# Column sums on the vector engines for two modulation banks, rows spread by DMA, C blocks without context

## The chip, the core and the metric

The kernel runs on one core of a Trainium2 chip. The core has five engines with a queue each: TensorE (PE in the profile, with its weight loads as PEld), VectorE (DVE), ScalarE (ACT), GpSimd (POOL) and SyncE (SP), which here only issues DMAs. ACT and POOL issue some DMAs too. Each engine works through its queue in order and waits at semaphores for the others. The metric is the device time of one execution in microseconds. Before the change the median of three runs is 1828.47 us (1827.12 to 1831.48).

## The reference

One layer of a hybrid diffusion backbone in float32, with 512 latent tokens `x`, 256 context tokens `ctx` and model width 1024. What matters here is the modulation, the projection and the convolution:

```python
mod = jax.nn.silu(c) @ ada_w[i] + ada_b[i]
sh1, sc1, g1, sh2, sc2, g2 = jnp.split(mod[:, None, :], 6, axis=-1)
mod_c = jax.nn.silu(c_ctx) @ ada_w[i] + ada_b[i]
csh1, csc1, cg1, csh2, csc2, cg2 = jnp.split(mod_c, 6, axis=-1)
...
zc, xbcc, dtc, poolc, qc, kc, vc = project(hc, csh1, csc1, norm1_g[i], w_in[i])
ssd_c, st_f, st_b = ssd_mixer(zc, xbcc, dtc, *ssd_args, None, None, need_ctx_out)
...
z, xbc, dtr, pl, q, k, v = project(h, sh1, sc1, norm1_g[i], w_in[i])
ssd_l, _, _ = ssd_mixer(z, xbc, dtr, *ssd_args, st_f, st_b, True)
...
h = h + g1 * mix
u = rmsnorm(h, norm2_g[i]) * (1 + sc2) + sh2
h = h + g2 * peer_ffn(u, ...)
```

`project` is an RMSNorm with `(1 + scale)` and `shift`, times `w_in`. `xbc` has 1536 columns, twelve blocks of 128: eight of x, two of B and two of C. They go through a centred convolution of three taps over the tokens and a SiLU. The context is used for the final states of the scan and for the keys and values of the attention; the states need x, B and dt, and with one layer (`need_ctx_out` false) nothing reads C of the context tokens. `mod` has 6144 values for the latent tokens. Its first third, sh1 and sc1, is needed for both kinds of tokens; the rest, g1, sh2, sc2 and g2, for the latent ones alone. The mixers' outputs go through one output projection, and `peer_ffn` is an expert layer over 128 x 128 experts.

## The kernel before

All projections are float32 products made of three passes: ACT rounds a weight tile to its high half (`split`, L177), DVE or POOL subtracts to get the low half (L180), and PE multiplies high by high, high by low and low by high (`mm3`, L187 to L189; `mm_xc`, L402 to L407, for latent and context columns together: 512 and 256 columns for the same weights).

**Stages.** First the start, with an order written out by hand (`START`): the input norm, its transposes, the first third of the modulation, and the first three xBC blocks. Then the rest of the first projection, which the planner orders: nine more xBC blocks (`for cb in range(12)`), four pooling blocks, four K blocks, and V of the context (`projC`). Then, again in a written order, the rest of the projection with the scan; the attention with the first half of the output projection (step numbers `O0 + n`); the second half, in which only PE's order is left to the program; norm2; the search of keys; and the expert stage from about 600 us to the end.

**Weights.** Each projection block loads 512 KB on SP's queue (`wload`, L208) into a ring of three raw tiles and splits it into a ring of two pairs of halves.

**The later modulation.** `ada_bank(bank, pool)` makes columns 2048 to 4095 (bank 1: g1, sh2) or 4096 to 6143 (bank 2: sc2, g2). It is a generator: each `next(ada)` of the block loops makes it take one slice of 128 rows of `ada_w` (two DMAs of 512 KB on SP into the tiles `xin`, which are pieces of kT, qT and vc not in use yet) and issue four matmuls of `cc` (128 x 32, whose columns 0 and 1 are the two conditions) by 512 columns, one in each column strip of the array (L478). The eight slices are summed in one PSUM bank, which puts piece j of the bank at partition 32 j. Then DVE adds the bias into `mod` (L482), four transposes bring the columns to partitions (L485), and DVE writes `sh2T` (L493) or `sc2T` (L497). `next(ada)` stands behind the projection of every xBC block, pooling block and K block.

**Rows.** g1, sc2, sh2 and g2 are also needed along the free dimension on all partitions. `row_bc` does that with a selecting matrix in the constants (C_SEL, 512 columns): two matmuls (L1133) and two ACT copies (L1135) for each row of 1024. It is called for `g1r` at step O0 + 66 of the attention stage, for `bcr` and `bcr2` between two weight pieces of the output projection's second half, and for `g2r` in the expert stage at i = 64 (`f_load`). `g1r` is first read by `out_end` behind that stage, `bcr` and `bcr2` make the copy `u2G` of one token block in norm2, and `g2r` is read in the last expert steps.

**The conv.** For each xBC block ACT copies the projection into `xp` (L563 latent, L564 context), DVE does the three taps on 770 columns (L566 to L568), ACT the SiLU. For the C blocks (cb 10 and 11) only the first 512 columns are kept.

Of the kernel before, what the change touches and what calls it, by code (L numbers as in the profile page):

```python
# [7 lines left out]
F32 = mybir.dt.float32  # L8
# [9 lines left out]
P = 128  # L18
# [19 lines left out]
KVAR = (0, 1, 1, 2)  # L38


C_ID, C_U, C_L, C_SU, C_SL, C_ONE, C_SEL = 0, 128, 256, 384, 512, 640, 768
NCST = C_SEL + 4 * 128


def _consts():
    c = np.zeros((P, NCST), np.float32)
    k = np.arange(P)[:, None]
    m = np.arange(P)[None, :]
    c[:, C_ID:C_ID + P] = k == m
    c[:, C_U:C_U + P] = k <= m  # L50
    c[:, C_L:C_L + P] = k >= m
    c[:, C_SU:C_SU + P] = k > m
    c[:, C_SL:C_SL + P] = k < m
    c[:, C_ONE:C_ONE + P] = 1.0
    for j in range(4):
        c[32 * j, C_SEL + j * P:C_SEL + (j + 1) * P] = 1.0
    return c


# [91 lines left out]
def build(tc, A, out, dbg=None):  # L151
# [97 lines left out]
    h_d = tc.dram_tile([SEQ, D], F32, name="h_d")  # L249
    gd_d = tc.dram_tile([NQ, P, P, TQ], F32, name="gd_d")  # L250
    act_d = tc.dram_tile([len(AHEAD), P, TD], F32, name="act_d")

    def rstd_of(pool, ssq, n, width):

# [185 lines left out]
    def projT(src, with_ctx=True):  # L440

        h, l = wspl(wload(kpc(src)), KB)
        px = psG.tile([P, 512], F32, name="acc")
        pc = psG.tile([P, 512], F32, name="acc") if with_ctx else None
        for k in range(KB):
            if with_ctx:
                mm_xc(px, pc[:, :CTX], h, l, k)
            else:
                mm3(px, h[:, k, :], l[:, k, :], uh[:, k, :], ul[:, k, :], k == 0, k == KB - 1)
        return px, pc  # L450

    def projC(c0):

        accs = [psG.tile([P, 512], F32, name="acc") for _ in range(NT - NX)]
        for kk in range(4):
            h, l = wspl(wload(kpc(A["w_in"][kk * 256:(kk + 1) * 256, c0:c0 + 512])), 2)
            for t, acc in enumerate(accs):
                for k2 in range(2):
                    k = kk * 2 + k2
                    mm3(acc, uch[:, k, t * P:(t + 1) * P], ucl[:, k, t * P:(t + 1) * P],  # L460
                        h[:, k2, :], l[:, k2, :], k == 0, k == KB - 1)
        return accs
# [4 lines left out]
    def ada_bank(bank, pool):  # L467

        adab = pool.tile([P, 512], F32, name="adab")
        nc.scalar.dma_start(adab, A["ada_b"][:, (bank - 1) * 512:bank * 512])  # L470
        ps = psG.tile([P, 512], F32, name="acc")
        for k in range(KB):
            for jj in range(2):
                w = xin[(2 * k + jj) % NT]
                nc.sync.dma_start(w, A["ada_w"][k * P:(k + 1) * P, (bank - 1) * 2048 + jj * 1024:(bank - 1) * 2048 + (jj + 1) * 1024])
                for j2 in range(2):
                    j = jj * 2 + j2
                    PE.matmul(ps[32 * j:32 * j + 32, :], cc[:, k, :], w[:, j2 * 512:(j2 + 1) * 512],  # L478
                              start=k == 0, stop=k == KB - 1, tile_position=(0, 32 * j))
            yield None  # L480
        m = mod[:, bank - 1, :]
        V.tensor_tensor(m, ps, adab, ALU.add)  # L482
        pt = psT.tile([P, 4, P], F32, name="pt")
        for q in range(4):
            PE.transpose(pt[:, q, :], m[:, q * P:(q + 1) * P], ident)  # L485

        yield pt.rearrange("p m (j r) -> p j m r", r=32)

    def ada_rest():

        for r in ada_bank(1, ad1):
            if r is not None:
                V.tensor_copy(jm(sh2T), r[:, 2:4, :, 0])  # L493
            yield
        for r in ada_bank(2, ad1):
            if r is not None:
                V.scalar_tensor_tensor(jm(sc2T), r[:, 0:2, :, 0], 1.0, jm(n2g), ALU.add, ALU.mult)  # L497
            yield
    ada = ada_rest()
    cvp = Pools()  # L500
    tp = cvp.sb("tmpC", bufs=2, side="right")
# [55 lines left out]
    for cb in range(12):  # L557
        if cb in (1, 4, 5):
            next(dtp, None)
        px, pc = early[cb] if cb < 3 else projT(A["w_in"][:, XBC0 + cb * P:XBC0 + (cb + 1) * P])  # L560
        next(ada, None)
        xp = xps[cb % 2]
        S.activation(xp[:, 1:513], px, AF.Copy)  # L563
        S.activation(xp[:, 515:771], pc[:, :CTX], AF.Copy)  # L564
        c1 = tp.tile([P, 770], F32, name="c1")
        V.tensor_scalar(c1, xp[:, 1:771], convw[:, 12 + cb:13 + cb], convb[:, cb:cb + 1], ALU.mult, ALU.add)  # L566
        V.scalar_tensor_tensor(c1, xp[:, 0:770], convw[:, cb:cb + 1], c1, ALU.mult, ALU.add)
        V.scalar_tensor_tensor(c1, xp[:, 2:772], convw[:, 24 + cb:25 + cb], c1, ALU.mult, ALU.add)  # L568
        if cb >= 10:
            S.activation(CT[:, cb - 10, :], c1[:, :SEQ], AF.Silu)  # L570
            continue
        sT = tp.tile([P, 770], F32, name="sT") if cb < 8 else BT[:, cb - 8, :]
        S.activation(sT, c1, AF.Silu)
        dst = xsn[:, :, cb * P:(cb + 1) * P] if cb < 8 else Bn[:, :, (cb - 8) * P:(cb - 7) * P]
        pt = psT.tile([P, 4, P], F32, name="pt")
        for j in range(4):
            PE.transpose(pt[:, j, :], sT[:, j * P:(j + 1) * P], ident)
        V.tensor_copy(dst[:, 0:4, :], pt)
        pt = psT.tile([P, 4, P], F32, name="pt")
        for j in range(2):  # L580
            PE.transpose(pt[:, j, :], sT[:, 514 + j * P:514 + (j + 1) * P], ident)
        S.activation(dst[:, 4:6, :], pt[:, 0:2, :], AF.Copy)
# [42 lines left out]
    for b in range(4):  # L625
# [3 lines left out]
        next(ada, None)  # L629
        if pend:  # L630
            pool_out(*pend.pop(0))
    for t, acc in enumerate(projC(V0)):
        V.tensor_copy(vc[:, t, :], acc)
    plp.close()
    adp.close()
# [17 lines left out]
    def at(step, f, *a):  # L653
        plan.setdefault(step, []).append((f, a))
# [471 lines left out]
    pso = Pools()  # L1126
    psO = pso.ps("psO", bufs=4)

    def row_bc(dst, ps_of, bank, j0):

        for j in range(2):
            ps = ps_of()
            PE.matmul(ps, cst[:, C_SEL + (j0 + j) * P:C_SEL + (j0 + j + 1) * P], mod[:, bank - 1, :],  # L1133
                      start=True, stop=True)
            S.activation(dst[:, j * 512:(j + 1) * 512], ps, AF.Copy)  # L1135

    def out_mm(acc, w, kk, t, first, last):
        for k2 in range(2):
# [12 lines left out]
    for i in range(2, 12):  # L1151
        before(O0 + OI[i], i_high, i)
        at(O0 + OI[i], i_low, i)
    at(O0 + 66, row_bc, g1r, lambda: psS.tile([P, 512], F32, name="sps"), 1, 0)

    def o_first(low):
        for t in range(NX):
# [69 lines left out]
    for i, kk in enumerate((4, 5, 0, 1, 2)):  # L1227
        w = out_w(kk, 1)
        if i == 2:
            row_bc(bcr, psu, 2, 0)  # L1230
            row_bc(bcr2, psu, 1, 2)
            G.tensor_tensor(bcr, bcr, n2row, ALU.mult)
            G.tensor_tensor(bcr, bcr, n2row, ALU.add)
        for t in range(NX):
            out_mm(accs[t], w, kk, t, i == 0, False)
# [526 lines left out]
    def f_load():  # L1762

        nc.sync.dma_start(fgr, A["rowg"][:, D:2 * D])
        row_bc(g2r, psu, 2, 2)

    hx = {}

# [148 lines left out]
```

## Time and profile before

| | |
|---|---|
| median of the runs | 1828.47 us |
| the profiled execution, its own time | 1827.76 us |
| its span, first to last instruction | 1826.0 us |
| mean granted TensorE clock | 0.993 |
| DMA traffic | 453.56 MB, 248 GB/s in the mean |
| expert weights, ut and uv | 128 loads of 512 KB each |

The page counts an engine as busy while an instruction runs on it; register, wait and DMA-issuing instructions are not counted. A row of a group gives line, engine, operation, written and read tiles, shape and count. A row of waits gives the waiting engine with its tile and line, what it waited for, the total in us, how often, and the longest. In a timeline the columns are start and length in us, and merged rows carry their count. A matmul in plain float32 (L478, L1133) shows as two records; a three-pass product shows each pass as one.

| line | what | records | mean us |
|---|---|---|---|
| L478 | modulation matmuls, 32 x 512 | 128 | 0.60 |
| L1133 | row matmuls, 128 x 512 | 16 | 0.59 |
| L1135 | ACT copies of the rows | 8 | 0.60 |
| L567, L568 | conv taps on DVE, 770 columns | 24 | 1.02 |

### The profile page before, as it was taken

To read this page: it belongs to the slowest core of one execution; us is meant where nothing else is said; L and a number is where in the kernel's file an instruction comes from. 1 tells how busy PE (TensorE), PEld (TensorE's weight loads), DVE (VectorE), ACT (ScalarE), POOL (GpSimd) and SP (SyncE) were. 2 spreads that over 40 slices of the span, in tenths; PEclk is the share of its full clock that TensorE was granted. 3 is DMA by queue.
4 is the path that set the end of the run, shared out by engine and by line. 5 is a ranking of instruction groups with operands and counts; after the bars stand their busy time and mean duration, and the time that the engine had idled before them with its cause. 6 is when DMAs were issued, how large, how long until landed. Compare 5 with 4: busy or idle time off the path is not lost.

```text
span 1826.0 us, 26332 instructions
## 1 busy us (share of the span) xinstructions
PE 1784.9 (98%) x9703; PEld 1511.1 (83%) x9703; DVE 1350.0 (74%) x2574; ACT 848.9 (46%) x1506; POOL 393.6 (22%) x276
## 2 busy tenths in 40 slices
PE   6999999999999999999999999999999999999997
PEld 4677777667677988999999998888888888888885
DVE  5554147876544569988999987988888888888876
ACT  4433245455554433355777673444344344444444
POOL 1100400252223634400111111211111111111103
PEclk9999999999999999999999999999999999999999
DMA  9545432148332633575999989999999899999971
GB/s 372 175 143 164 120 92 70 58 160 282 107 99 95 185 112 110 147 260 164 366 345 343 333 307 396 398 353 341 367 344 353 336 347 385 350 348 344 365 245 55
DMA packets 191457, 453.56 MB, mean 248 GB/s; under 512 B 13632, under 2 KB 117312, under 8 KB 173376
## 3 DMA queue, kind: packets, MB, share of 16 engines
q1 hardware_dynamic: 147120, 259.51, 42.1%
q0 software_dynamic: 18576, 136.32, 19.6%
q10 hardware_dynamic: 25632, 56.04, 8.3%
q8 instruction: 76, 1.25, 0.3%
q14 instruction: 53, 0.43, 0.1%
HBM read 399.27 MB, written 54.66 MB: 249 GB/s over the span
## 4 chain that ended last, share of the span: by engine, by line
PE 81%; DVE 2%; ACT 1%; issue 1%; DMA 1%; POOL 0%; ACTq 0%; SPq 0%; DVEq 0%; POOLq 0%
PE pu L187 10%; PE pu L189 10%; PE pu L188 10%; PE pv L189 9%; PE pv L188 9%; PE pv L187 9%; PE acc L187 4%; PE acc L189 4%; PE acc L188 4%; PE mm L827 2%; PE gdps L1636 1%; PE gdps L1637 1%; PE sps L1029 1%; PE mm L769 1%; PE pt L1059 1%; PE acc L1436 1%
## 5 line engine op out<-in xcount | busy, mean ns | idle before, releaser
L180 DVE TENSOR_TENSOR wl<-wraw,wh 128x1024 fp32r<-128x1024 f32 x294 | 362.9, 1247 | 168.3 <-ACT wh L177 166.1
L177 ACT ACTIVATE wh<-wraw 128x1024 fp32r<-128x1024 f32 x328 | 341.1, 1052 | 206.1 <-PE acc L188 73.3
L187 PE MATMUL pu<-u2h,wh 128*128 128x384 f32 x1024 | 349.7, 342 | 0.0
L188 PE MATMUL pu<-u2l,wh 128*128 128x384 f32 x1024 | 344.8, 337 | 0.8 <-DVE u2l L180 0.8
L189 PE MATMUL pu<-u2h,wl 128*128 128x384 f32 x1024 | 345.4, 337 | 0.0
L1575 POOL DMA_INDIRECT row<-in_peer_uv,idxG x128 | 156.8, 1225 | 807.0 <-DVE accG L1589 713.0
L188 PE MATMUL pv<-wl,wwh 128*128 128x512 f32 x768 | 300.7, 392 | 2.3 <-DVE wl L180 2.2
L187 PE MATMUL pv<-wh,wwh 128*128 128x512 f32 x768 | 301.7, 393 | 0.4 <-ACT wh L177 0.3
L189 PE MATMUL pv<-wh,wwl 128*128 128x512 f32 x768 | 300.9, 392 | 0.0
L188 PEld LDWEIGHTS pu<-u2l,wh 128*128 128x128 f32 x1024 | 192.5, 188 | 2.9 <-DVE u2l L180 1.1
L187 PEld LDWEIGHTS pu<-u2h,wh 128*128 128x128 f32 x1024 | 192.3, 188 | 1.8
L189 PEld LDWEIGHTS pu<-u2h,wl 128*128 128x128 f32 x1024 | 192.2, 188 | 0.6 <-DVE wl L180 0.5
L188 PEld LDWEIGHTS pv<-wl,wwh 128*128 128x128 f32 x768 | 144.2, 188 | 34.1 <-DVE wl L180 3.8
L189 PEld LDWEIGHTS pv<-wh,wwl 128*128 128x128 f32 x768 | 144.2, 188 | 32.2
L187 PEld LDWEIGHTS pv<-wh,wwh 128*128 128x128 f32 x768 | 144.3, 188 | 31.1 <-ACT wh L177 1.2
L1589 DVE SCALAR_TENSOR_TENSOR accG<-row,wG,accG 128x1024 f32<-128x1024 f32 x127 | 162.4, 1278 | 4.7 <-ACT wG L1584 3.4
L1580 DVE CUSTOM_DVE_ANT_0 row<-row,u2G 128x1024 f32<-128x1024 f32 x128 | 155.0, 1218 | 0.0
L177 ACT ACTIVATE wwh<-acl 128x384 fp32r<-128x384 f32 x86 | 45.2, 526 | 203.6 <-DVE acl L1748 136.0
L1639 ACT ACTIVATE stg<-gdps 128x512 f32<-128x512 f32 x96 | 101.6, 1172 | 19.7 <-PE gdps L1637 18.1
L180 POOL TENSOR_TENSOR wl<-wraw,wh 128x1024 fp32r<-128x1024 f32 x34 | 81.6, 2406 | 102.4 <-ACT wh L177 70.9
L1742 ACT ACTIVATE act<-pu 128x384 f32<-128x384 f32 x42 | 20.6, 491 | 156.7 <-PE pu L189 156.7
L1748 DVE TENSOR_TENSOR act<-act,gd 128x384 f32<-128x384 f32 x42 | 23.4, 558 | 84.2 <-ACT act L1742 84.2
(414 smaller groups left out, 3121.7 us busy)
## 6 DMA issues: line engine op xcount, KB each, us to landing
wraw<-in_peer_ut SPq DMA_DIRECT2D x128, 512.0 KB, 5.7
wraw<-in_peer_uv SPq DMA_DIRECT2D x128, 512.0 KB, 8.4
gd<-gd_d SPq DMA_DIRECT2D x15, 1536.0 KB, 13.8
gd_d<-stg ACTq DMA_DIRECT2D x11, 2048.0 KB, 8.6
wraw<-in_w_in SPq DMA_DIRECT2D x40, 512.0 KB, 4.1
acl<-act_d SPq DMA_DIRECT2D x86, 192.0 KB, 5.9
act_d<-act ACTq DMA_DIRECT2D x84, 192.0 KB, 5.0
kT<-in_ada_w SPq DMA_DIRECT2D x18, 512.0 KB, 5.1
```

What stands on the lines that cost most here:

```text
L177: S.activation(hi, full, AF.Copy)
L180: (eng or V).tensor_tensor(lo, full, hi.bitcast(F32), ALU.subtract)
L187: PE.matmul(ps, ah, bh, start=start, stop=False)
L188: PE.matmul(ps, ah, bl, start=False, stop=False)
L189: PE.matmul(ps, al, bh, start=False, stop=stop)
L827: PE.matmul(ps, m, ms[d].rearrange("p a b -> p (a b)"), start=d == 0, stop=d == 1)
L1575: G.indirect_dma_start(out=rows[k], out_offset=None, in_=A["peer_uv"], in_offset=bass.IndirectOffsetOnAxis(ap=idxG[:, k:k + 1], axis=0))
L1580: V.tensor_tensor_reduce(row[:, 0:D], row[:, 0:D], u2G, 1.0, 0.0, ALU.mult, ALU.add, actG[:, k:k + 1])
L1589: V.scalar_tensor_tensor(accG, row[:, D:2 * D], wG[:, k:k + 1], accG, ALU.mult, ALU.add)
L1639: S.activation(stg[:, :, t0:t0 + 4].rearrange("p a t -> p t a"), ps, AF.Copy, scale=1.0 / GSCALE)
L1742: S.activation(ac[a], pu[:, :TD], AF.Gelu)
L1748: V.tensor_tensor(xq, xq, gds.pop(a), ALU.mult)
```

## The change

The sum over a bank's 1024 rows is no longer made by accumulating matmuls. For each slice, the 128 x 1024 tile is multiplied by the condition's value of its partition and added to a tile `part` (128 x 2048): by DVE in one instruction, and for the first half of bank 1 by ACT (multiply in place) and POOL (add). At the end of a bank four matmuls with a matrix of ones add up the 128 partitions of `part`, into the same places as before. Only the latent condition is summed. The finished bank is also stored to a DRAM tile `mod_d` by four DMAs of 2 KB on SP's queue.

`next(ada)` is now called from block cb = 4 on, behind the conv taps instead of ahead of them, in every pooling and K block, and once more behind the V matmuls; the step that finishes a bank goes on at once with the next bank's first slice. From slice 12 of the 16 on, the loads use only the three tiles of qT and vc.

`row_bc` is one DMA that reads 1024 values of `mod_d` for each of the 128 partitions. For `g1r` it is issued on ACT's queue at step O0 + 16, for `bcr` and `bcr2` on ACT's queue at the old place, for `g2r` on SP's queue. The selecting matrix leaves the constants, whose second load shrinks from 576 to 320 KB.

The C blocks project only the latent columns, with `mm3`, and their conv works on 512 columns.

```diff
--- before.py
+++ after.py
@@ -38,8 +38,8 @@
 KVAR = (0, 1, 1, 2)
 
 
-C_ID, C_U, C_L, C_SU, C_SL, C_ONE, C_SEL = 0, 128, 256, 384, 512, 640, 768
-NCST = C_SEL + 4 * 128
+C_ID, C_U, C_L, C_SU, C_SL, C_ONE = 0, 128, 256, 384, 512, 640
+NCST = 768
 
 
 def _consts():
@@ -52,8 +52,6 @@
     c[:, C_SU:C_SU + P] = k > m
     c[:, C_SL:C_SL + P] = k < m
     c[:, C_ONE:C_ONE + P] = 1.0
-    for j in range(4):
-        c[32 * j, C_SEL + j * P:C_SEL + (j + 1) * P] = 1.0
     return c
 
 
@@ -249,6 +247,7 @@
     h_d = tc.dram_tile([SEQ, D], F32, name="h_d")
     gd_d = tc.dram_tile([NQ, P, P, TQ], F32, name="gd_d")
     act_d = tc.dram_tile([len(AHEAD), P, TD], F32, name="act_d")
+    mod_d = tc.dram_tile([2, 4, 512], F32, name="mod_d")
 
     def rstd_of(pool, ssq, n, width):
 
@@ -468,18 +467,30 @@
 
         adab = pool.tile([P, 512], F32, name="adab")
         nc.scalar.dma_start(adab, A["ada_b"][:, (bank - 1) * 512:bank * 512])
+        part = pool.tile([P, 2048], F32, name="adac")
+        for k in range(KB):
+            n = (bank - 1) * KB + k
+            for jj in range(2):
+                w = xin[(2 * n + jj) % NT] if n < 12 else xin[3 + (2 * n + jj) % 3]
+                nc.sync.dma_start(w, A["ada_w"][k * P:(k + 1) * P, (bank - 1) * 2048 + jj * 1024:(bank - 1) * 2048 + (jj + 1) * 1024])
+                dst, ck = part[:, jj * 1024:(jj + 1) * 1024], cc[:, k, 0:1]
+                if jj == 0 and bank == 1:
+                    S.activation(w if k else dst, w, AF.Copy, scale=ck)
+                    if k:
+                        G.tensor_tensor(dst, dst, w, ALU.add)
+                elif k:
+                    V.scalar_tensor_tensor(dst, w, ck, dst, ALU.mult, ALU.add)
+                else:
+                    V.tensor_scalar(dst, w, ck, None, ALU.mult)
+            yield None
         ps = psG.tile([P, 512], F32, name="acc")
-        for k in range(KB):
-            for jj in range(2):
-                w = xin[(2 * k + jj) % NT]
-                nc.sync.dma_start(w, A["ada_w"][k * P:(k + 1) * P, (bank - 1) * 2048 + jj * 1024:(bank - 1) * 2048 + (jj + 1) * 1024])
-                for j2 in range(2):
-                    j = jj * 2 + j2
-                    PE.matmul(ps[32 * j:32 * j + 32, :], cc[:, k, :], w[:, j2 * 512:(j2 + 1) * 512],
-                              start=k == 0, stop=k == KB - 1, tile_position=(0, 32 * j))
-            yield None
+        for j in range(4):
+            PE.matmul(ps[32 * j:32 * j + 32, :], ONE[:, 0:32], part[:, j * 512:(j + 1) * 512],
+                      start=True, stop=True, tile_position=(0, 32 * j))
         m = mod[:, bank - 1, :]
         V.tensor_tensor(m, ps, adab, ALU.add)
+        for j in range(4):
+            nc.sync.dma_start(mod_d[bank - 1, j:j + 1, :], m[32 * j:32 * j + 1, :])
         pt = psT.tile([P, 4, P], F32, name="pt")
         for q in range(4):
             PE.transpose(pt[:, q, :], m[:, q * P:(q + 1) * P], ident)
@@ -489,13 +500,15 @@
     def ada_rest():
 
         for r in ada_bank(1, ad1):
-            if r is not None:
+            if r is None:
+                yield
+            else:
                 V.tensor_copy(jm(sh2T), r[:, 2:4, :, 0])
-            yield
         for r in ada_bank(2, ad1):
-            if r is not None:
+            if r is None:
+                yield
+            else:
                 V.scalar_tensor_tensor(jm(sc2T), r[:, 0:2, :, 0], 1.0, jm(n2g), ALU.add, ALU.mult)
-            yield
     ada = ada_rest()
     cvp = Pools()
     tp = cvp.sb("tmpC", bufs=2, side="right")
@@ -557,17 +570,21 @@
     for cb in range(12):
         if cb in (1, 4, 5):
             next(dtp, None)
-        px, pc = early[cb] if cb < 3 else projT(A["w_in"][:, XBC0 + cb * P:XBC0 + (cb + 1) * P])
-        next(ada, None)
+        px, pc = early[cb] if cb < 3 else projT(A["w_in"][:, XBC0 + cb * P:XBC0 + (cb + 1) * P], cb < 10)
         xp = xps[cb % 2]
         S.activation(xp[:, 1:513], px, AF.Copy)
-        S.activation(xp[:, 515:771], pc[:, :CTX], AF.Copy)
-        c1 = tp.tile([P, 770], F32, name="c1")
-        V.tensor_scalar(c1, xp[:, 1:771], convw[:, 12 + cb:13 + cb], convb[:, cb:cb + 1], ALU.mult, ALU.add)
-        V.scalar_tensor_tensor(c1, xp[:, 0:770], convw[:, cb:cb + 1], c1, ALU.mult, ALU.add)
-        V.scalar_tensor_tensor(c1, xp[:, 2:772], convw[:, 24 + cb:25 + cb], c1, ALU.mult, ALU.add)
+        n = SEQ
+        if cb < 10:
+            S.activation(xp[:, 515:771], pc[:, :CTX], AF.Copy)
+            n = 770
+        c1 = tp.tile([P, 770], F32, name="c1")[:, :n]
+        V.tensor_scalar(c1, xp[:, 1:n + 1], convw[:, 12 + cb:13 + cb], convb[:, cb:cb + 1], ALU.mult, ALU.add)
+        V.scalar_tensor_tensor(c1, xp[:, 0:n], convw[:, cb:cb + 1], c1, ALU.mult, ALU.add)
+        V.scalar_tensor_tensor(c1, xp[:, 2:n + 2], convw[:, 24 + cb:25 + cb], c1, ALU.mult, ALU.add)
+        if cb >= 4:
+            next(ada, None)
         if cb >= 10:
-            S.activation(CT[:, cb - 10, :], c1[:, :SEQ], AF.Silu)
+            S.activation(CT[:, cb - 10, :], c1, AF.Silu)
             continue
         sT = tp.tile([P, 770], F32, name="sT") if cb < 8 else BT[:, cb - 8, :]
         S.activation(sT, c1, AF.Silu)
@@ -629,7 +646,9 @@
         next(ada, None)
         if pend:
             pool_out(*pend.pop(0))
-    for t, acc in enumerate(projC(V0)):
+    accs = projC(V0)
+    next(ada, None)
+    for t, acc in enumerate(accs):
         V.tensor_copy(vc[:, t, :], acc)
     plp.close()
     adp.close()
@@ -1126,13 +1145,10 @@
     pso = Pools()
     psO = pso.ps("psO", bufs=4)
 
-    def row_bc(dst, ps_of, bank, j0):
-
-        for j in range(2):
-            ps = ps_of()
-            PE.matmul(ps, cst[:, C_SEL + (j0 + j) * P:C_SEL + (j0 + j + 1) * P], mod[:, bank - 1, :],
-                      start=True, stop=True)
-            S.activation(dst[:, j * 512:(j + 1) * 512], ps, AF.Copy)
+    def row_bc(dst, bank, j0, queue):
+
+        row = mod_d[bank - 1, j0:j0 + 2, :].rearrange("j c -> (j c)").unsqueeze(0)
+        queue.dma_start(dst, row.broadcast_to([P, D]))
 
     def out_mm(acc, w, kk, t, first, last):
         for k2 in range(2):
@@ -1151,7 +1167,7 @@
     for i in range(2, 12):
         before(O0 + OI[i], i_high, i)
         at(O0 + OI[i], i_low, i)
-    at(O0 + 66, row_bc, g1r, lambda: psS.tile([P, 512], F32, name="sps"), 1, 0)
+    at(O0 + 16, row_bc, g1r, 1, 0, nc.scalar)
 
     def o_first(low):
         for t in range(NX):
@@ -1227,8 +1243,8 @@
     for i, kk in enumerate((4, 5, 0, 1, 2)):
         w = out_w(kk, 1)
         if i == 2:
-            row_bc(bcr, psu, 2, 0)
-            row_bc(bcr2, psu, 1, 2)
+            row_bc(bcr, 2, 0, nc.scalar)
+            row_bc(bcr2, 1, 2, nc.scalar)
             G.tensor_tensor(bcr, bcr, n2row, ALU.mult)
             G.tensor_tensor(bcr, bcr, n2row, ALU.add)
         for t in range(NX):
@@ -1762,7 +1778,7 @@
     def f_load():
 
         nc.sync.dma_start(fgr, A["rowg"][:, D:2 * D])
-        row_bc(g2r, psu, 2, 2)
+        row_bc(g2r, 2, 2, nc.sync)
 
     hx = {}
 
```

## The prediction

> **What bounds the kernel now.** I read the page's busy shares and slices first, then TensorE's waits in the second part of the run, then the table by stage.
>
> ```profile
> PE 1784.9 (98%) x9703; PEld 1511.1 (83%) x9703; DVE 1350.0 (74%) x2574; ACT 848.9 (46%) x1506; POOL 393.6 (22%) x276
> ...
> PEclk9999999999999999999999999999999999999999
> DMA  9545432148332633575999989999999899999971
> ```
>
> The first row is the busy share, the others the granted clock and the DMA share in 40 slices. PE is busy 98% of the span, but its ends are modelled, so the share alone does not say that it is the bound. The waits do. From 600 to 1800 us, the whole expert stage, the view of PE's waits has a single row, and that row is 0.8 us; over the whole run these rows concern the stages up to the first projection's end:
>
> ```profile
> PE pv L188 <- DVE wl L180: 0.8, 1, 0.8
> ...
> PE acc L404 <- POOL ul L180: 2.6, 3, 1.2
> PE mm L731 <- ACT enF L733: 1.4, 1, 1.4
> PE mm L731 <- DVE vc L633: 0.9, 1, 0.9
> ```
>
> No DMA is named in any row of that view. The table by stage agrees:
>
> ```profile
> 100.00:140.00 40.00, 40.00 (x246) 32.38 (x246) 23.70 (x39) 15.14 (x23) 0.00 (x0) 1.00 0.49 158
> 174.00:208.00 34.00, 34.00 (x171) 22.99 (x170) 6.20 (x6) 9.48 (x13) 23.01 (x20) 1.00 0.63 190
> 220.00:260.00 40.00, 37.55 (x181) 30.86 (x180) 11.95 (x17) 12.22 (x21) 3.76 (x2) 0.96 0.33 98
> 1200.00:1400.00 200.00, 200.00 (x940) 172.98 (x939) 165.28 (x215) 83.21 (x160) 33.71 (x31) 1.00 0.94 347
> ```
>
> The columns are PE, PEld, DVE, ACT, POOL, granted clock, DMA share and GB/s. PE has no pause where the change works (100 to 208 us), nor later at a DMA share of 0.94. So whatever leaves PE's instruction stream before 600 us should pull the end forward by as much, unless a new wait takes its place.
>
> **Part 1: later modulation banks off PE.** L478 issues 64 matmuls; each shows as two records. First the table of windows for L478 alone, then the timeline around one group.
>
> ```profile
> 66.00:70.00 4.00, 2.78 (x22) 0.66 (x22) 1.00 1.16 304
> 80.00:210.00 130.00, 13.85 (x104) 2.05 (x104) 1.00 0.51 154
> ```
>
> ```profile
> 80.75 0.28 PE L407 MATMUL acc<-uch,wl 128*128 128x256 f32 x1
> 80.96 1.07 PE L478 MATMUL acc<-kT,cc 128*32 128x512 f32 x8
> 81.96 0.33 PE L525 MATMUL acc<-ucl,whl 128*64 128x256 f32 x1
> ```
>
> The 104 records between 80 and 210 us are 13 groups of eight, one for each slice of 128 rows. From start to next start a group takes 81.96 - 80.96 = 1.00 us. The start before it comes 0.21 us ahead instead of the 0.12 of such a matmul, and the one behind costs some 0.05 more, so I count 1.14 us: 13 x 1.14 = **14.8 us**. A mean duration (0.59 us) times 128 would say 76 us and be wrong, as four column strips run side by side. The Trainium skill (TensorE: Matmul & The Clock Gate, Part 3) makes a pack of column tiles about one matmul long plus 4 ns per tile; by it a group of two packs would be 1.19 us, and the sum 13 x 0.05 = 0.7 us larger. The measured starts decide.
>
> The other 24 records stand where PE had to wait anyway, by the timeline:
>
> ```profile
> 57.67 1.28 POOL L180 TENSOR_TENSOR ul<-uf,uh 128x512 fp32r<-128x512 f32 x1 [5.96 <-ACT uh L177]
> 57.93 1.30 DVE L180 TENSOR_TENSOR ucl<-uf,uch 128x256 fp32r<-128x256 f32 x1 [0.68 <-ACT uch L177]
> 58.26 1.04 PE L478 MATMUL acc<-kT,cc 128*32 128x512 f32 x2
> ...
> 66.86 1.48 PE L478 MATMUL acc<-kT,cc 128*32 128x512 f32 x9
> 68.77 1.21 DVE L180 TENSOR_TENSOR wl<-wraw,wh 128x1024 fp32r<-128x1024 f32 x1
> 69.57 0.50 PE L402 MATMUL acc<-uh,wh 128*128 128x512 f32 x1
> ```
>
> The two at 58.26 fill a wait for ul, which POOL has ready at 58.95: I take nothing (0 to 1.0). The 22 from 66.86 to 69.57 (2.71 us) stand ahead of a block whose low half is only ready at 69.98; the projection matmuls for dt (L525) are ready and can fill, so I take **1.8** (0 to 2.7).
>
> The four matmuls that sum over partitions are two records each, eight to a bank: two groups, **-2.3**. The sums go to DVE, ACT and POOL. The nearest rows, of single lines and groups, and then of the waits between 55 and 250 us:
>
> ```profile
> L1589 DVE SCALAR_TENSOR_TENSOR accG<-row,wG,accG x127: 1272/1278/1289, 870.3 to 1761.5; 128x1024 f32<-128x1024 f32 x127
> L177 ACT ACTIVATE wh<-wraw 128x1024 fp32r<-128x1024 f32 x328 | 341.1, 1052 | 206.1 <-PE acc L188 73.3
> L180 POOL TENSOR_TENSOR wl<-wraw,wh x34: 2383/2405/2432, 567.8 to 769.7; 128x1024 fp32r<-128x1024 f32 x34
> ```
>
> ```profile
> ACT wh L177 <- PE acc L405: 54.0, 12, 7.4
> ```
>
> DVE gets 24 operations, at most 24 x 1.28 = 30.7 us over some 150; ACT 8 copies of the kind of L177 (1.05 us); POOL 7 x 2.41 = 16.9 us. DVE's 23.70 of 40 us leaves room, and the weight splits wait for PE to free their buffers (54.0 us in 12 waits), a block ahead of use. This cover is thinnest in the C and pooling blocks, which last 24 matmuls of 0.23 = 5.5 us without their modulation group. There I allow **-2.5** (0 to -14, the second rival).
>
> **Part 2: C blocks without context.** Two blocks lose 8 x 3 matmuls of 256 columns each.
>
> ```profile
> 79.48 0.39 PE L406 MATMUL acc<-uh,wl 128*128 128x512 f32 x1
> 79.71 0.28 PE L407 MATMUL acc<-uch,wl 128*128 128x256 f32 x1
> 79.83 0.39 PE L402 MATMUL acc<-uh,wh 128*128 128x512 f32 x1
> ```
>
> 512 columns take 0.23 us to the next start. From L407 here to L407 at 80.75, quoted above, three such pairs start in 1.04 us, 0.347 a pair, so 256 columns are worth 0.117: 48 x 0.117 = **5.6**. DVE and ACT get shorter conv work too, which nobody waits for.
>
> **Part 3: rows by DMA.** L1133's matmuls go: four calls, four records each. The timeline of the first, and two DMA issues of the size that takes their place:
>
> ```profile
> 521.05 1.88 PE L1133 MATMUL sps<-mod,cst 128*128 128x512 f32 x4
> 522.37 0.80 PE L187 MATMUL acc<-wh,mAh 128*128 128x512 f32 x1
> 523.00 0.40 PE L188 MATMUL acc<-wl,mAh 128*128 128x512 f32 x1
> ```
>
> ```profile
> h<-in_x ACTq DMA_DIRECT2D x4, 512.0 KB, 6.5
> fgr<-in_rowg SPq DMA_DIRECT2D x1, 512.0 KB, 14.1
> ```
>
> 1.32 us, and the next matmul starts its follower 0.63 us later instead of 0.23: 1.72 x 4 = **6.9**. PE has no pause around any of the four, so all of it counts. In place come four DMAs of 512 KB (6.5 and 14.1 us to landing in these rows): g1r is issued 50 steps of the written order ahead of its use, bcr and bcr2 144 matmuls of 0.23 us ahead, g2r half the expert stage ahead. That work hides them, and I cost them at nothing; without it, a late one would cost at most its landing time, 6.5 us. The eight 2 KB stores and their waits for m sit on SP's queue; behind them stand weight loads that have a block or more in hand. The constants load shrinks by 256 KB; no row of PE's waits names a DMA, so nothing (0 to 0.8, from the 347 GB/s of the quoted stage).
>
> **Part 4: the end of the first projection.** The second bank used to end in the middle of the K blocks. Now it ends behind V: sum matmuls, add, four transposes, the write of sc2T, then PSUM passes to the next stage.
>
> ```profile
> 245.20 1.28 DVE L633 COPY vc<-acc 128x512 f32<-128x512 f32 x2
> 246.53 0.69 PE L731 MATMUL mm<-an,cst 128*128 128x96 f32 x4 [0.89 <-DVE vc L633]
> 248.66 1.49 PE L731 MATMUL mm<-an,cst 128*128 128x96 f32 x8 [1.45 <-ACT enF L733]
> ```
>
> That chain is about 3 us by estimate: 1.0 for a group of eight as above, 0.64 for an add of 512 columns (half of the row of two copies), twice the 0.69 of four small matmuls for the eight records of the transposes. PE idles 0.9 + 1.4 us here already, so most of it can lie in that gap: **-0.8** (+0.9 to -3).
>
> **Sum.** 14.8 + 1.8 - 2.3 - 2.5 + 5.6 + 6.9 - 0.8 = 23.5 us. The profiled run took 1827.76 us (span 1826.0), 0.7 below the median of 1828.47. 1827.76 - 23.5 = 1804.3, and from the median 1805.0; I say **1804.5 us**.
>
> **The rivals.**
>
> *The shared port eats the gain.* The rows at 57.67 and 57.93 show it: 128x256 on DVE takes 1.30 us beside a POOL operation and ends with the next free moment after it, while the fastest row of that kind takes 0.42.
>
> ```profile
> L180 DVE TENSOR_TENSOR ucl<-uf,uch x8: 416/1298/1508, 23.3 to 60.7; 128x256 fp32r<-128x256 f32 x8
> ```
>
> So DVE and POOL take turns when both read two tensors from SBUF. In the four pooling blocks POOL works 23.0 us; DVE would have 4 x (1.21 + 2 x 1.28) = 15.1. Strictly in turn that is 38 us in 22 us of PE work. The rest can run on under the K blocks, yet each weight split waits in DVE's order behind two sums, and the pooling matmul of L599 behind POOL. If half of that surplus of 16 us reaches PE, the time is 1804.5 + 8 - 2.5 = 1810; if all, 1818. For it: the rows. Against it: a block's lead on every split, and four K blocks of 24 x 0.347 = 8.3 us with a nearly idle DVE. The Trainium skill (SBUF — State Buffer, Who interferes with whom) has the rule, an exclusive lock on the pair of ports; the trace agrees at 1.30 against 0.42. **17%**, 1810 to 1818.
>
> *A cold clock behind V.* If the chain of part 4 isn't covered, PE stands for about 2 us more. The table gives 0.96 of the clock in 220 to 260 us, 1.6 us lost, after 2.3 us of idling. Twice that loss and 2 us of idling make +3.6: 1808. By the Trainium skill (TensorE: Matmul & The Clock Gate, Part 1) an idle window of about 3.4 us halves the clock; the 0.96 beside a shorter wait agrees in kind. **5%**.
>
> *Absorbed.* The expert stage is bound by DMA (0.94), and an earlier start changes nothing: 1828. Against it: one wait of 0.8 us in 1200 us. **3%**.
>
> *Slower: a jam on SP's queue.*
>
> ```profile
> SPq L475 <- PE acc L478: 80.6, 12, 14.0
> SPq L208 <- DVE wl L180: 69.0, 16, 10.1
> ```
>
> SP takes weight and modulation loads in order, and waits up to 14 us for a modulation buffer. Now a buffer comes free after ACT and POOL (1.05 + 2.41 = 3.46 us) instead of a matmul group, and three buffers serve the K blocks instead of six. If the weights behind come late by that in each of 16 steps, 55 us are lost: 1860. It decides from 23.5 / 16 = 1.5 us a step. Against it: weight loads now wait 69.0 us for their own buffers, so they are early. **5%**.
>
> *The change doesn't do what it says:* the 1.0 us per slice returns because ACT or DVE sets the block's period. The 54.0 us for which ACT waits for PE speak against it; its price, 14.8, falls in the first rival's range, and so does its chance.
>
> **How the numbers follow.** Forecast 70%, its own range 1797 to 1810 (best ends of all terms: about 1797). The 80% range takes in the lock: 1796 to 1818. What a measurement of this kernel can tell from no change is about 0.2%, 3.7 us. Faster 0.70 + 0.17 + 0.05 = 0.92, same 0.03, slower 0.05.
>
> **What would show it.** Right: no matmul of 128*32 but 16 records, PE's waits between 70 and 245 us still under 3 us, no L1133, C blocks 5.5 us long, the expert stage starting some 22 us earlier and lasting as long. Wrong: rows PE <- DVE wl or PE <- POOL in the pooling and K blocks (the lock), a low clock after V, ACT wh <- DMA wraw (the jam), or PE pauses at DVE tiles that wait for g1r.

## The result, and the profile after

The changed kernel takes 1815.46 us (median of four runs, 1814.57 to 1817.15) against 1827.8 us for the kernel before in the same series; the ratio is 0.9932 with an interval of [0.9916, 0.9947]. It is faster by about 12 us. The prediction was 1804.5 us with a range of 1796 to 1818: the sign and the wide range held, the gain is little more than half of the 23.5 us forecast, and the time lies outside the forecast's own range of 1797 to 1810. In the series below, one execution of the kernel with the sums alone took 3537.91 us; its ratio is taken without it.

The busy shares on the page of the changed kernel:

```profile
PE 1757.7 (97%) x9527; PEld 1501.0 (83%) x9527; DVE 1405.2 (78%) x2598; ACT 850.5 (47%) x1504; POOL 424.6 (23%) x283
```

PE is busy 27.2 us less (1784.9 - 1757.7), but the span shrank by only 13.2 (1826.0 to 1812.8). So the work did leave PE, and about half of the time came back as idling. PE's waits between 55 and 250 us, first before the change, then after:

```profile
PE mm L731 <- ACT enF L733: 1.4, 1, 1.4
PE mm L731 <- DVE vc L633: 0.9, 1, 0.9
PE acc L404 <- POOL ul L180: 0.7, 1, 0.7
```

```profile
PE pt L594 <- ACT sT L590: 8.0, 3, 5.0
PE acc L187 <- DVE wl L178: 1.6, 1, 1.6
PE mm L750 <- ACT enF L752: 1.4, 1, 1.4
PE acc L403 <- POOL ul L178: 1.3, 2, 0.7
PE acc L405 <- DVE wl L178: 1.3, 1, 1.3
PE pt L496 <- DVE mod L491: 0.8, 1, 0.8
```

The new first row is 8.0 us: the transposes of a conv block (L594) wait for its SiLU, once for 5.0 us. The two rows with wl are weight splits: 1.6 us in a pooling block (at 178.21) and 1.3 us in the first K block (at 192.70), where POOL still works on the pooling. The first of the lines below is before, the others after, from the table by stage (PE, PEld, DVE, ACT, POOL, granted clock, DMA share, GB/s):

```profile
60.00:100.00 40.00, 39.14 (x237) 29.09 (x236) 21.26 (x34) 17.48 (x30) 1.27 (x1) 1.00 0.65 201
```

```profile
60.00:100.00 40.00, 31.16 (x166) 25.23 (x167) 36.72 (x40) 23.94 (x35) 16.95 (x7) 0.90 0.68 216
174.00:208.00 34.00, 31.12 (x150) 24.82 (x149) 32.59 (x16) 8.18 (x12) 32.46 (x19) 1.00 0.80 244
220.00:260.00 40.00, 37.62 (x180) 29.00 (x179) 18.53 (x26) 15.79 (x34) 3.76 (x2) 1.00 0.32 93
```

The reader should compare the counts in brackets with the busy times. Between 60 and 100 us DVE has six instructions more than before (40 against 34) and is busy 15.46 us longer. Six instructions of at most 1.28 us are 7.7 us, so the instructions themselves became longer, while POOL worked 16.95 us in the same window. The timeline there, in order of start, shows how:

```profile
74.24 2.95 DVE L484 TENSOR_SCALAR adac<-kT,cc 128x1024 f32<-128x1024 f32 x1
74.24 2.40 POOL L480 TENSOR_TENSOR adac<-adac,kT 128x1024 f32<-128x1024 f32 x1 [11.69 <-ACT kT L478]
...
76.72 2.73 POOL L480 TENSOR_TENSOR adac<-adac,qT 128x1024 f32<-128x1024 f32 x1
77.12 3.16 DVE L582 SCALAR_TENSOR_TENSOR c<-xp,colv,c 128x770 f32<-128x770 f32 x1
...
79.53 2.94 POOL L480 TENSOR_TENSOR adac<-adac,kT 128x1024 f32<-128x1024 f32 x1
80.20 0.68 DVE L595 COPY xsn<-pt 128x512 f32<-128x512 f32 x1
80.80 2.49 DVE L583 SCALAR_TENSOR_TENSOR c<-xp,colv,c 128x770 f32<-128x770 f32 x1
...
83.38 0.85 ACT L590 ACTIVATE sT<-c 128x770 f32<-128x770 f32 x1 [4.39 <-DVE c L583]
...
84.28 0.47 PE L594 MATMUL pt<-cst,sT 128*128 128x128 f32 x1 [5.04 <-ACT sT L590]
```

A conv tap that took 1.02 us before (the table of the front part) starts at 77.12, while POOL's addition of 76.72 runs until 79.45, and ends at 80.28, 0.83 us after POOL. The second tap starts at 80.80 inside the addition that ends at 82.47 and ends at 83.29, again 0.82 behind it. ACT's SiLU, the transposes and all that PE has in order behind them wait for that. The copy out of PSUM between them takes its usual 0.68 us. So DVE's two-input instruction ends only when POOL's addition has ended: the mechanism of the first rival, but in the xBC blocks, where the prediction didn't look for it.

### The profile page after: what moved, and what is told of

The parts are those of the page before. It is cut to its first block, busy times and chain, and to the rows that moved or that the text cites. A ratio compares the mean times of both kernels' runs of the same rounds, so it can differ in the third digit from the quotient of the medians.

```text
span 1812.8 us, 26042 instructions
## 1 busy us (share of the span) xinstructions
PE 1757.7 (97%) x9527; PEld 1501.0 (83%) x9527; DVE 1405.2 (78%) x2598; ACT 850.5 (47%) x1504; POOL 424.6 (23%) x283
## 4 chain that ended last, share of the span: by engine, by line
PE 87%; DVE 4%; ACT 3%; issue 2%; DMA 2%; POOL 1%; SPq 0%; ACTq 0%; DVEq 0%; POOLq 0%
PE pu L185 10%; PE pu L187 9%; PE pu L186 9%; PE pv L187 9%; PE pv L186 9%; PE pv L185 9%; PE acc L185 5%; PE acc L187 5%; PE acc L186 5%; PE mm L846 2%; PE gdps L1652 1%; PE gdps L1653 1%; PE acc L403 1%; PE acc L401 1%; PE acc L405 1%
## 5 line engine op out<-in xcount | busy, mean ns | idle before, releaser
L178 DVE TENSOR_TENSOR wl<-wraw,wh 128x1024 fp32r<-128x1024 f32 x294 | 367.4, 1262 | 109.0 <-ACT wh L175 106.1
```

Source lines behind the costliest of these rows:

```text
L178: (eng or V).tensor_tensor(lo, full, hi.bitcast(F32), ALU.subtract)
```

## Experiments

All ratios are to the kernel before, run on the same chip beside it; its medians were 1827.21 us (first series: the parts alone, and who does the sums), 1829.37 (second: the sums alone, the K blocks, the late row and both) and 1830.16 (third: C blocks and rows together, and the last pair). The theory under test: DVE instructions with two inputs in SBUF and POOL instructions take turns, and this eats the sums' gain. Its rivals put the loss into the rows by DMA, into the loads, or into DVE's work as such.

**The C blocks alone, on the kernel before** (the line below, and the shorter conv as in the change).

```diff
-        px, pc = ... projT(A["w_in"][:, XBC0 + cb * P:XBC0 + (cb + 1) * P])
+        px, pc = ... projT(A["w_in"][:, XBC0 + cb * P:XBC0 + (cb + 1) * P], cb < 10)
```

> The kernel before with the C blocks' context columns left off, nothing else. My sum gave this part 5.6 us (48 matmuls of 256 columns at 0.117). Theory (each removed matmul is paid back in full, since TensorE has no pause there): 5 to 6.5 us below the kernel before. Rival (the block period is set by something else, so the part is worth less): under 3 us.

1820.31 us, ratio 0.9964 [0.9944, 0.9985]: a gain of 6.6 us (2.7 to 10.2), where 5.6 was forecast.

**The rows alone, on the kernel before** (the stores of `mod`, four row DMAs, no selecting matrix).

```diff
-            PE.matmul(ps, cst[:, C_SEL + (j0 + j) * P:...], mod[:, bank - 1, :], ...)
-            S.activation(dst[:, j * 512:(j + 1) * 512], ps, AF.Copy)
+        queue.dma_start(dst, row.broadcast_to([P, D]))
```

> The kernel before with the four rows spread by DMA from a stored copy of the modulation, nothing else. My sum gave 6.9 us. Theory: the copy of the rows now lands some 30 us earlier, POOL works on bcr beside the end of the first half of the output projection, and a TensorE pause of about 1.6 us appears at the first matmuls of the second half; so 4.5 to 6 us below the kernel before, with that pause in the trace. Rival (all of it is paid back): 6.9 us and no pause.

1822.0 us, ratio 0.9971 [0.996, 0.9982]: 5.3 us (3.3 to 7.3) of the 6.9 forecast. Its view of PE's waits has a row that the kernel before lacks:

```profile
PE acc L185 <- DVE otmp L1215: 1.6, 1, 1.6
```

The pause is as long as the 1.6 us between 6.9 and 5.3, though the interval alone doesn't exclude 6.9. Its cause comes with the late rows below.

**The sums alone, on the kernel before** (its `ada_bank` and its calls replaced by those of the change).

```diff
-                    PE.matmul(ps[32 * j:32 * j + 32, :], cc[:, k, :], w[:, j2 * 512:(j2 + 1) * 512], ...)
+                if jj == 0 and bank == 1:
+                    S.activation(w if k else dst, w, AF.Copy, scale=ck)
+                    if k:
+                        G.tensor_tensor(dst, dst, w, ALU.add)
+                elif k:
+                    V.scalar_tensor_tensor(dst, w, ck, dst, ALU.mult, ALU.add)
```

> The kernel before with the modulation sums of the change alone (ACT and POOL for the first half of bank 1): rows by matmul and context in the C blocks as before. My sum gave this part 14.8 + 1.8 - 2.3 - 2.5 - 0.8 = 11.0 us. Theory (what it takes off TensorE comes back as waits, since DVE and POOL hold each other up): within 3 us of the kernel before, with pauses of 5 us or more between 74 and 101 us. Rival (the parts disturb each other only in combination): 8 us or more below the kernel before.

1827.56 us, ratio 0.9992 [0.9975, 1.001]: nothing that can be told from zero, where the prediction's terms for this part add up to 14.8 + 1.8 - 2.3 - 2.5 - 0.8 = 11.0. The waits of PE in this kernel:

```profile
PE pt L593 <- ACT sT L589: 8.0, 2, 5.1
...
PE acc L406 <- DVE wl L180: 1.4, 1, 1.4
...
PE acc L189 <- DVE wl L180: 1.2, 1, 1.2
```

The same pauses as in the whole change, so neither the C blocks nor the rows make them.

**C blocks and rows, without the sums.** The two edits above together.

> The kernel before with the C blocks for latent tokens alone and the rows by DMA; the modulation sums stay as single matmuls. If the sums split between ACT and POOL are worth nothing (0.9992 [0.9975, 1.001] for them alone), this kernel is as fast as the whole change: 6.9 + 5.5 us below before, 1814 to 1818, ratio about 0.993. Rival: the three parts help each other (a row that leaves by DMA needs its bank early, which the sums give), and the sums are worth some 5 us within the change: then 1819 to 1823. No PE pause of over 2 us between 60 and 110 us in either.

1815.57 us, ratio 0.9927 [0.9914, 0.9941], against 0.9932 for the whole change: taking the sums out of the change alters nothing that these intervals can tell. The measured gain is that of the two other parts.

**Without POOL's additions.** From the changed kernel the seven additions go. The first half of bank 1 (g1) then holds only its first slice (not the last, as the expectation says), so the result is wrong and only the time counts; the rest is as in the change.

```diff
                     S.activation(w if k else dst, w, AF.Copy, scale=ck)
-                    if k:
-                        G.tensor_tensor(dst, dst, w, ALU.add)
```

> The changed kernel without POOL's seven additions in bank 1; the first half of bank 1 (g1) is left out of the sum but for its last slice's products, so the output differs. DVE's work is the same. Theory (DVE and POOL take turns at SBUF, and the additions hold up the conv taps between 74 and 101 us): the taps take 1.02 us again, TensorE's two pauses of 5.0 and 2.8 us at the transposes shrink to under 2 us together, the half clock behind them goes, and the time is 7 to 11 us below the changed kernel, 1804 to 1809. Rival (DVE has simply more to do in these blocks than fits): the pauses stay over 5 us and the time is within 3 us of the changed kernel's 1815.

1805.91 us, ratio 0.9887 [0.9862, 0.9911]: 9.6 us below the change, as the theory said. Its row of the table by stage:

```profile
60.00:100.00 40.00, 38.44 (x223) 31.96 (x224) 32.48 (x45) 26.57 (x39) 1.41 (x2) 1.00 0.79 266
```

The clock is 1.00 again, PE's waits at the transposes are 0.5 us in all instead of 8.0, and the taps take 1.01 to 1.02 us. ACT's multiplications are still there, so they aren't the cause.

**All sums on DVE.** Nothing is left out here: ACT's multiplications and POOL's additions become DVE instructions.

```diff
-                if jj == 0 and bank == 1:
-                    S.activation(w if k else dst, w, AF.Copy, scale=ck)
-                    if k:
-                        G.tensor_tensor(dst, dst, w, ALU.add)
-                elif k:
+                if k:
                     V.scalar_tensor_tensor(dst, w, ck, dst, ALU.mult, ALU.add)
```

> The changed kernel with bank 1 summed wholly on DVE: ACT's copies and POOL's additions go, DVE gets eight more operations of 1.28 us. Theory (turns between DVE and POOL): although DVE has 10 us more to do, its tap rows take 1.02 us again between 74 and 101 us, the two pauses of 7.8 us shrink to under 4, and the time is 4 to 9 us below the changed kernel, 1806 to 1811. Rival (DVE's load): the pauses grow beyond 8 us, and the time is above 1815.

1804.85 us, ratio 0.9877 [0.9857, 0.9898]: some 10 us better than the change, a little more than the theory named, with *more* work on the engine that was late. Its row of the table by stage, and two taps from its timeline:

```profile
60.00:100.00 40.00, 38.55 (x225) 32.44 (x226) 37.18 (x50) 17.62 (x30) 1.63 (x2) 1.00 0.71 227
```

```profile
75.45 1.01 DVE L578 SCALAR_TENSOR_TENSOR c<-xp,colv,c 128x770 f32<-128x770 f32 x1
...
76.98 1.01 DVE L579 SCALAR_TENSOR_TENSOR c<-xp,colv,c 128x770 f32<-128x770 f32 x1
```

Sixteen instructions more than before take 15.92 us more, 1.0 each; in the change six took 15.46. DVE is as busy as in the change and PE gets 38.55 instead of 31.16 us. A busy DVE isn't the cause, then; together with the run before, POOL's additions beside it are. The two runs win back 9.6 and 10.6 us; the two pauses and the half clock behind them, counted in the next section, make 7.8 + 3.8 = 11.6. Against C blocks and rows without sums (0.9927), the sums on DVE are worth 0.0050 of the time, about 9 us.

**No sums in the pooling blocks, two in each K block** (on the kernel with all sums on DVE; the loads use the three late tiles from slice 8 on).

```diff
-                w = xin[(2 * n + jj) % NT] if n < 12 else xin[3 + (2 * n + jj) % 3]
+                w = xin[(2 * n + jj) % NT] if n < 8 else xin[3 + (2 * n + jj) % 3]
 # pooling blocks
-        next(ada, None)
 # K blocks
         next(ada, None)
+        next(ada, None)
```

> Bank 1 on DVE alone, and no step of the sums called in the pooling blocks; the K blocks call two each, through the ring of three tiles. Theory (in the pooling blocks DVE and POOL take turns, so DVE's low halves come late): the two pauses of 1.6 and 1.3 us at wl in the pooling blocks go, wl takes 1.2 us there instead of 2.1 to 2.3, and the time is 1.5 to 4 us below bank 1 on DVE alone (1804.9), 1801 to 1803.5. Rival (the pauses come from DVE's load): they move to the K blocks and the time stays within 1 us. If the planner moves sums of the ring's first tiles up into the pooling blocks, one of the pauses may stay.

1805.02 us, ratio 0.9866 [0.9844, 0.9887]: no gain over all sums on DVE. The pauses of the pooling blocks are gone, but PE now waits for wl in the V projection. DVE's timeline there, and PE's:

```profile
215.13 1.28 DVE L478 SCALAR_TENSOR_TENSOR adac<-qT,cc,adac 128x1024 f32<-128x1024 f32 x1 [1.28 <-DMA qT<-in_ada_w]
216.34 1.22 DVE L178 TENSOR_TENSOR wl<-wraw,wh 128x1024 fp32r<-128x1024 f32 x1
```

```profile
217.60 0.80 PE L186 MATMUL acc<-wl,uch 128*128 128x512 f32 x1 [2.47 <-DVE wl L178]
```

A weight split stands in DVE's order behind a sum that waits for its tile to arrive. The load moved, and it met another limit.

**The row of bcr held back** (on the kernel with all sums on DVE). Copying one element per partition of the last finished `h` into each row's tile makes the DMA wait for the residual.

```diff
+            for r in (bcr, bcr2):
+                V.tensor_copy(r[:, 0:1], h[:, 3, 0:1])
             row_bc(bcr, 2, 0, nc.scalar)
```

> Bank 1 on DVE alone, and the row DMA of bcr held until the third token block's first half of the output projection is added (one element copied into bcr ahead of the DMA). Theory (POOL's two early operations on bcr hold up DVE's and POOL's work at the end of the first half): the pause of 1.5 us at the first matmuls of the second half goes, and the time is 1 to 2 us below bank 1 on DVE alone, about 1803.4. Rival (the pause is the price of the missing row matmuls, whatever POOL does): the pause stays at 1.5 us.

1801.8 us, ratio 0.985 [0.983, 0.987]. First the timeline of the changed kernel at that place, then POOL's in this kernel:

```profile
521.17 2.41 POOL L1248 TENSOR_TENSOR bcr<-bcr,xn 128x1024 f32<-128x1024 f32 x1 [9.31 <-PE acc L187]
523.66 3.26 POOL L1249 TENSOR_TENSOR bcr<-bcr,xn 128x1024 f32<-128x1024 f32 x1
526.88 2.51 POOL L1234 TENSOR_TENSOR h<-h,otmp 128x512 f32<-128x512 f32 x2
...
529.71 0.50 PE L185 MATMUL acc<-wh,mBh 128*128 128x512 f32 x1 [1.62 <-DVE otmp L1233]
```

```profile
510.41 2.54 POOL L1230 TENSOR_TENSOR h<-h,otmp 128x512 f32<-128x512 f32 x2 [10.92 <-DVE otmp L1229]
513.25 2.54 POOL L1230 TENSOR_TENSOR h<-h,otmp 128x512 f32<-128x512 f32 x2 [0.31 <-DVE otmp L1229]
522.87 2.40 POOL L1246 TENSOR_TENSOR bcr<-bcr,xn 128x1024 f32<-128x1024 f32 x1 [7.08 <-DMA bcr<-mod_d]
```

In the change the row's two POOL operations run at once and the residual `h`, for which PE's PSUM buffers wait, stands behind them in POOL's order. In the kernel before, `h` came first too (at 532.74, bcr at 548.73). Here `h` goes first again, and the view of PE's waits has no such row any more. The pause explains 1.6 us of the gain; the times differ by 3 us, 1801.8 against 1804.85, in two series and with intervals that overlap, so the rest isn't shown.

**Both.** The edits of the last two together.

> Bank 1 on DVE alone with both edits: no steps in the pooling blocks, and bcr's row late. Theory: both gains add, 4.4 us of pauses go, 1800 to 1802.5; with the best ends of my sum at 1797 as the floor. Rival: no better than the better one of the two.

1807.7 us (1801.01 to 1809.25), ratio 0.9867 [0.9844, 0.989]: the pauses in V are there again (3.8 us in two waits for wl), and the rival held.

**Sums of the pooling blocks done earlier** (on the kernel with bcr held back), beside a second run of that kernel.

```diff
         if cb >= 4:
             next(ada, None)
+        if cb in (6, 7, 8, 9):
+            next(ada, None)
 # pooling blocks
-        next(ada, None)
```

> dve_late without any step in the four pooling blocks; their steps are done in the column blocks 6 to 9, one extra in each, where DVE has about 11 of 40 us free. If the pauses of 1.5 and 1.3 us in the pooling blocks come from VectorE and GpSimd taking turns, both go, none comes in the V projection, and the time is 1 to 3 us below that of dve_late on the same chip, ratio 0.983 to 0.985. Rival: VectorE's two steps in a block (about 2.6 us more) make it late for the taps of the next block: new pauses of over 2 us in all between 100 and 150 us, and a time equal to that of dve_late or above it.

> The same kernel as dve_late, for a comparison with dve_spread on one chip: 0.985 [0.983, 0.987] before, so 1799 to 1804 here by either theory.

1809.89 us, ratio 0.9896 [0.9877, 0.9914], against 1801.6 us, 0.9848 [0.9832, 0.9863], for the second run of the kernel with bcr held back. The theory's number failed and the rival held, a little later than named. DVE's timeline, and the matmul that waited:

```profile
153.75 1.28 DVE L478 SCALAR_TENSOR_TENSOR adac<-qT,cc,adac 128x1024 f32<-128x1024 f32 x1
...
154.94 1.27 DVE L478 SCALAR_TENSOR_TENSOR adac<-vc,cc,adac 128x1024 f32<-128x1024 f32 x1
156.14 0.54 DVE L577 TENSOR_SCALAR c<-xp,colv 128x512 f32<-128x512 f32 x1
156.59 1.21 DVE L178 TENSOR_TENSOR wl<-wraw,wh 128x1024 fp32r<-128x1024 f32 x1
...
157.86 0.79 PE L187 MATMUL acc<-uh,wl 128*128 128x512 f32 x1 [2.82 <-DVE wl L178]
```

No POOL operation runs here and every duration is undisturbed. The steps fall together in the C blocks, which at 24 matmuls are as short as the pooling blocks, and the split waits behind them. From 156 to 164 us the mean granted clock is 0.57. One pause in the pooling blocks stayed as well (1.49 us at 172.86): steps still run there beside POOL, and wl takes 2.33 us. DVE's free time is at 100 to 140 us (it is busy 28.16 of 40), but its order put the sums elsewhere.

## Why the prediction was right in sign and half wrong in size

**The step that failed** is the term -2.5 of Part 1, with the sentence before it that DVE's 23.70 of 40 us leaves room. It was taken in a range of 0 to -14, near the mild end. In the changed kernel's profile the pauses are 5.04 and 2.76 us in the xBC blocks and 1.57 and 1.30 in the pooling blocks and the first K block, 10.7 in all. The clock was halved in the course of the first and behind it, and behind the second:

```profile
81.60:88.40 6.80, 4.12 (x16) 3.30 (x16) 6.76 (x7) 4.33 (x7) 1.09 (x2) 0.50 0.59 210
98.70:102.10 3.40, 3.40 (x13) 2.92 (x12) 3.40 (x2) 1.30 (x2) 3.23 (x2) 0.50 0.88 313
```

PE worked 4.12 + 3.40 us there at a clock of 0.50 (a matmul of 512 columns at 85.84 starts its follower 0.43 us later, instead of 0.23), which costs half of it, 3.8 us. Together -14.5 stands where -2.5 was allowed: 12.0 us, about the whole miss of 11. The error was to add up durations as each engine shows them alone. DVE's free 16 us of 40 were counted as room, and POOL's 16.9 us as work off the path, though the prediction had quoted the very rows (1.30 against 0.42 us) by which the two can't run at once. By windows: DVE 21.26 us before, plus 6 sums (7.7), plus POOL's 16.95 in turn, is 45.9 us of 40. That is an upper estimate, as not all of DVE's 21.26 us are two-input instructions.

**The first rival had the mechanism, but in the wrong place and for the wrong bank.** It was priced for the pooling blocks, with bank 2; 1810 to 1818 came out of that and 1815.46 lies in it. But there only 2.9 us were lost, so that the time fell into this range is luck. The larger part, 7.8 us and the half clock, came in the xBC blocks from POOL's additions of bank 1. Its 17%, against 70% for the forecast, looked at the pooling blocks alone. The Trainium skill (SBUF — State Buffer, Who interferes with whom) says that a VectorE instruction with two SBUF inputs contends with a GpSimd instruction that reads SBUF, and calls the shared pair of ports an exclusive lock. The traces agree: the five two-input instructions of DVE that start in an addition between 77 and 99 us end 0.81 to 1.09 us behind it. The rule was cited in the prediction, for the rival; it belonged in the sum.

**Confirmed by runs.** With all sums on DVE the time is 1804.85 us, a gain of 22.5 (18.6 to 26.1) where the sum gave 23.5: without POOL's additions the sum nearly holds. Partly that is chance: with the pauses of 2.9 us that stay, and the rows and Part 4 as measured, the sum is 14.8 + 1.8 - 2.3 - 2.9 + 5.6 + 5.3 - 1.3 = 21.0. C blocks: 6.6 measured, 5.6 forecast. Rows: 5.3 measured, 6.9 forecast; with the pause of 1.6 us added back the matmuls' price comes out, but "I cost them at nothing" failed, though not by a late DMA, as allowed for, but by an early one, which put POOL's work on bcr ahead of the residual.

**Part 4** was sized well. The end of V in the changed kernel:

```profile
238.39 0.39 PE L187 MATMUL acc<-wh,ucl 128*128 128x512 f32 x1
238.70 1.06 PE L488 MATMUL acc<-adac,cst 128*32 128x512 f32 x8
240.59 0.66 PE L496 MATMUL pt<-cst,mod 128*128 128x128 f32 x4 [0.82 <-DVE mod L491]
241.08 0.58 PE L750 MATMUL mm<-an,cst 128*128 128x96 f32 x4
243.11 1.49 PE L750 MATMUL mm<-an,cst 128*128 128x96 f32 x8 [1.45 <-ACT enF L752]
244.38 0.47 PE L185 MATMUL acc<-wh,uh 128*128 128x512 f32 x1
```

From the last V matmul to the next stage's first are 244.38 - 238.39 = 5.99 us, against 249.93 - 245.26 = 4.67 before (the row of L189 there starts at 245.26): -1.3 for the forecast -0.8. The cold clock behind V did not come in the profiled execution, whose window of 220 to 260 us has a clock of 1.00; in those of other kernels here it is 0.91 to 0.96.

**Absorbed, and the jam on SP's queue**, are refuted. A wait of PE for a DMA doesn't appear in any row, and the expert stage passes an earlier start on almost fully: its first matmul moved from 592.55 to 580.81 us, 11.7 earlier, and the span became 13.2 shorter, of which the g2r row inside that stage is about 1.7.

**What stays open.** The terms, as measured where a run measures them and as forecast otherwise (14.8 + 1.8 - 2.3 - 14.5 + 5.6 + 5.3 - 1.3 = 9.4), leave 3 us of the 12.3 between the medians unassigned. Half clock in two other places is as large: the profile before has a clock of 0.96 from 220 to 260 us and 0.83 from 400 to 420, 1.6 + 3.4 us lost; the one after has 1.00 and 0.94, 1.2 us lost. Other kernels here have other values there, so one profile of each can't settle it. Whether POOL's pooling work could be moved away from the sums was not tried; without sums beside it its two pauses went, but others came.

## What to carry to other kernels

Count VectorE's two-input instructions and GpSimd's tensor operations in a stage as the work of *one* engine: where they met in these traces their busy times added up, whatever each showed as free. Sharing a sum between the two was worth nothing that could be measured here, while giving all of it to VectorE, and holding back a row that had come too early, gave 1801.8 us (ratio 0.985 [0.983, 0.987]), better than both kernels. When work is moved from the bound engine, ask for each instruction it goes to what stands behind it in that engine's order: a weight split behind a sum that waits for its DMA, or a residual behind a row that nobody needs yet, stopped PE although no engine's average over the stage was at its limit.

## What was not expected of the hardware

- DVE made hardly any headway while POOL's addition ran, and a run of additions hit every two-input instruction that started in one: taps of 1.02 us took up to 3.16. Even a multiply with one tensor input (L484) took 2.95 where it takes 0.74 to 0.75 with POOL idle. In the pooling blocks the two alternate, here in order of start:

```profile
174.92 2.15 POOL L636 TENSOR_TENSOR pb<-pb,pl 128x512 f32<-128x512 f32 x1
175.85 2.31 DVE L178 TENSOR_TENSOR wl<-wraw,wh 128x1024 fp32r<-128x1024 f32 x1
177.61 1.46 POOL L629 TENSOR_TENSOR pa<-pl 128x527 f32<-128x527 f32 x1 [0.34 <-ACT pl L627]
178.08 2.08 DVE L482 SCALAR_TENSOR_TENSOR adac<-kT,cc,adac 128x1024 f32<-128x1024 f32 x1
179.16 1.92 POOL L633 TENSOR_TENSOR pb<-pa 128x524 f32<-128x524 f32 x1
180.08 2.08 DVE L482 SCALAR_TENSOR_TENSOR adac<-qT,cc,adac 128x1024 f32<-128x1024 f32 x1
```

- A pause of PE of only 2.76 us (up to 97.66) was followed by 3.4 us at half clock, from 98.7 on. In the pause of 5.04 us (up to 84.28) the clock fell at 81.6 and stayed at half for 6.8 us. The pauses of 1.57 and 1.30 us were followed by none. But before the change two pauses of 0.89 and 1.45 us, quoted in the prediction for the end of V, were followed by matmuls 0.42 us apart (from 250.72) instead of 0.23. So the length of a single pause doesn't decide it, and what does isn't shown here. By the Trainium skill (TensorE: Matmul & The Clock Gate, Part 1) the windows have a length of about 3.4 us and run freely; the lengths of 3.4 and 6.8 agree, the pause of 2.76 us is shorter than the one idle window that the page asks for. From the start of that pause (94.90) to the next projection matmul (98.30), with only the six transposes between, are 3.40 us; whether they count as work for the clock isn't shown here.
